# Solving DeltaNet's diagonal blocks on 128 partitions without DRAM

## The chip, the cores and the metric

One core of a Trainium2 chip runs the whole program. The metric is the time of one execution in device microseconds (us). The core has five engines that run side by side, each strictly in the order of its own instructions: TensorE (PE in the profile, with its weight loads as PEld), VectorE (DVE), ScalarE (ACT), GpSimd (POOL) and SyncE (SP), which here issues the loads of the weights. An instruction that needs another engine's result waits for a semaphore, and everything behind it on its engine waits too.

## What is computed

The reference is a trunk of four layers over 256 tokens with 1024 features: a pooling mixer, a gated DeltaNet, latent attention, and a pooling mixer again. The change lies in the second layer:

```python
L = jnp.where(strict, jnp.einsum('bhnid,bhnjd->bhnij', k_beta, k) * decay, 0.0)
A = jnp.eye(C, dtype=L.dtype) + L
rhs = jnp.concatenate([v_beta, k_beta * jnp.exp(g)[..., None]], axis=-1)
sol = lax.linalg.triangular_solve(A, rhs, left_side=True, lower=True)
...
attn = jnp.where(causal, jnp.einsum('bhnid,bhnjd->bhnij', q, k) * decay, 0.0)
```

There are 8 heads with keys of 128 and values of 256 numbers; q and k are the projection of the layer's input after a causal convolution over four tokens, a SiLU and a normalisation. The reference works in chunks of 64 tokens; the kernel in two of 128 (t = 0, 1), which gives the same result. So for each of 16 pairs of chunk and head a lower triangular matrix I + L of 128 x 128 has to be inverted or solved.

## The kernel before

**Projections.** `project` multiplies the layer's input with 512 columns of a weight matrix. `weights` loads two blocks of 128 rows at a time on SP's queue (L133, three `raw` buffers) and splits each block into a rounded part (`whi`, a cast on ACT, L149) and a rest (`wlo`, a subtraction on DVE, L150, or on POOL for the blocks named in `pool`); nine buffers of each are in use. PE then makes three products per block (L162). In the DeltaNet layer there are twelve such projections, which the list `order` (L673) strings together: g0 to g3 are gates, k0 and k1 keys, q0 and q1 queries, v0 to v2 values, V3 and c3 the two halves of the last values. d, a0, a1, s and i are the decays, the matrices L of four heads each (`lower`), the substitution and the inverses; u0 and u1 use the result.

**What happens to a projection.** DVE runs three taps of the convolution (L750) over PE's result, ACT starts it (L747) and closes with a SiLU (L787 for keys and queries, written to `kqT`; L902 for values). PE transposes the result into tokens by channels (L793, L906). For keys, DVE copies them to `ktok` (L799). `against` makes products of four heads with the keys (L806), and DVE multiplies each head with its scale and its decays `DT` (L813): this gives `LT`, L transposed, from the keys, and `attnT` from the queries.

**The solution.** `substitution` cuts each of the 16 matrices into four diagonal blocks of 32 x 32. Eight copies on SP's queue (L838) bring the 64 blocks from `LT` to DRAM (`d_l`), and one brings them back as `Lb` (L841), one block to a partition, so on 64 partitions. POOL then runs 31 pairs of steps (L846, L850): row r times the solved rows, subtracted from the rows below; the result is the inverse of the blocks, `Tb`. POOL's queue writes it to DRAM (`d_t`, L853) and reads it back in four copies onto the diagonal of `T` (L857). `inverses` puts the blocks together: DVE transposes T to `U` (L929), then PE, DVE and ACT run two stages, `pairs` (L938 to L947) and `whole` (L952 to L965), for t = 0 and 1, with small matmuls of 64 and 32 columns. `news` (L979) multiplies the values with U, and a chain over the heads ends the layer (L1004 to L1055), with the next projection, `layer_out`, beside it.

**Order.** The program is recorded in the order of the code and of the list `order`; a list scheduler then places the instructions of all engines by a model of their times, so an engine's instructions of neighbouring steps are interleaved. On the chip this order is fixed. Buffers are handed on in the same way: `kqT` of q1 is written into the buffer that `Lb` had, and waits for its last reader.

Of the kernel before, what the change touches and what calls it, by code (L numbers as in the profile page):

```python
# [42 lines left out]
def trunk(ctx: ExitStack, tc: tile.TileContext, x, positions, norm_g, pool_w_in, pool_w_grp,  # L43
# [566 lines left out]
    def gdn_setup():  # L610
# [35 lines left out]
        GC.update(utri=utri, maskT=maskT, m32=m32, half=half, tap=tap, bws=bws,  # L646
                  alog=alog, dtb=dtb)

    def gdn_layer(i, j, hT):
# [124 lines left out]
        def channels(dst, c0, hf, which):  # L774
# [13 lines left out]
            for c in range(0, 4, 2):  # L788
# [9 lines left out]
                if which == 0:  # L798
                    nc.vector.tensor_copy(ktok[:, h:h + 2, :], ps[:, 0])  # L799

        def against(dst, rhs, sf, hf, t):
# [3 lines left out]
            for b in range(4):  # L805
                nc.tensor.matmul(ps[:, b], lhsT=kT[hf][:, b, tt], rhs=rhs[hf][:, b, tt],  # L806
                                 start=True, stop=True)
            for b in range(4):
# [4 lines left out]
                nc.vector.scalar_tensor_tensor(  # L813
                    out=o, in0=v, scalar=sf[:, t, h:h + 1], in1=d, op0=ALU.mult, op1=ALU.mult)
# [17 lines left out]
        def substitution():

            d_l = dram.tile([M * Q, B * B], F32, name="d_l")
            lv = d_l.rearrange("(t m d) (r c) -> t d r m c", t=NT, d=Q, r=B)
            for t in range(NT):
                for d in range(Q):
                    nc.sync.dma_start(out=lv[t, d],  # L838
                                      in_=LT[t][d * B:(d + 1) * B, :, d * B:(d + 1) * B])
# [571 lines left out]
```

## Time and profile before

| | |
|---|---|
| median of 3 runs | 829.0 us (827.01 to 829.16) |
| profiled execution | 832.1 us, its span 830.4 us |
| mean clock of PE | 0.986 of full speed |
| instructions | 16162 |
| layer with the change | about 170 to 420 us of the span |

The span is the time from the first to the last instruction. Rows of the profile read: start and duration in us, engine, line of the kernel, operation, written and read tile, shapes, and how many such instructions were merged (x). In brackets stands how long the engine was idle before the instruction, and what it waited for. Rows of windows give the stretch, its length, then the busy time and the number of instructions of PE, PEld, DVE, ACT and POOL, and last PE's granted clock, the share of the DMA engines and their GB/s. Rows with `|` are groups: count, then busy time in us and the mean of one instruction in ns, then the idle time before them. PE's busy time contains overlaps, since matmuls are pipelined.

### The profile page before, as it was taken

What the parts mean: (1) busy time and instruction counts of PE and PEld (TensorE: products, weight loads), DVE (VectorE), ACT (ScalarE), POOL (GpSimd) and SP (SyncE); (2) the same over time, 40 slices, a digit from 0 to 9 for tenths busy, and PEclk for the clock granted to TensorE, in tenths of its full rate; (3) what the DMA queues carried; (4) which work ended last, traced back from release to release, by engine and by line L of the source; (5) the groups of instructions that cost most, each with busy time, mean ns of one, the idle gap of its engine ahead of it and who ended that gap; (6) DMA issues with size and microseconds to landing.
All of it is one profiled execution on the core that took longest, in us unless ns stands there. A gap on an engine that the chain in (4) does not pass through costs nothing.

```text
span 830.4 us, 16162 instructions
## 1 busy us (share of the span) xinstructions
PE 799.4 (96%) x5966; PEld 758.0 (91%) x5966; DVE 603.4 (73%) x1141; ACT 492.9 (59%) x993; POOL 159.8 (19%) x296
## 2 busy tenths in 40 slices
PE   8989999999898979999999999999999999999996
PEld 7989988989898978788989999999999989999996
DVE  4699887666987967356666678778877767877772
ACT  6665565567855655255566564666665565566662
POOL 2001100334236992023121112000000120000012
PEclk9999999999999989899999999999999999999998
DMA  6865666756655544303647786653552547576662
GB/s 204 224 180 167 193 209 210 221 153 195 193 135 180 163 139 118 124 12 115 187 125 224 231 180 185 192 164 102 153 175 80 179 143 214 183 223 202 202 204 51
DMA packets 109079, 139.90 MB, mean 168 GB/s; under 512 B 21316, under 2 KB 51208, under 8 KB 109000
## 3 DMA queue, kind: packets, MB, share of 16 engines
q1 hardware_dynamic: 106608, 137.12, 55.0%
q0 software_dynamic: 528, 1.58, 0.6%
q8 instruction: 47, 0.77, 0.4%
q10 hardware_dynamic: 1864, 0.17, 0.2%
q14 instruction: 32, 0.26, 0.1%
HBM read 137.27 MB, written 1.58 MB: 167 GB/s over the span
## 4 chain that ended last, share of the span: by engine, by line
PE 67%; DVE 11%; POOL 8%; DMA 8%; issue 4%; ACT 2%; SPq 0%; POOLq 0%; DVEq 0%; ACTq 0%
PE acc L162 53%; PE aux L162 7%; POOL pr L846 3%; DVE wlo L154 3%; POOL Tb L850 2%; DMA raw<-in_pool_w_out_dram 2%; DVE wlo L150 1%; DMA raw<-in_pool_w_in_dram 1%; DVE win L551 1%; DMA T<-d_t 1%; DMA Lb<-d_l 1%; DVE h L397 1%; DMA Gb<-d_g 1%; PE aux L979 1%; PE tp L1314 1%
## 5 line engine op out<-in xcount | busy, mean ns | idle before, releaser
L150 DVE TENSOR_TENSOR wlo<-raw,whi 128x512 fp32r<-128x512 f32 (+1 forms) x366 | 254.2, 719 | 104.3 <-ACT whi L149 100.8
L149 ACT CAST whi<-raw 128x512 fp32r<-128x512 f32 (+1 forms) x380 | 223.7, 617 | 167.6 <-PE acc L162 82.3
L162 PE MATMUL acc<-hTh,whi 128*128 128x256 f32 x832 | 230.7, 278 | 2.3 <-ACT gsg L670 1.5
L162 PE MATMUL acc<-hTl,whi 128*128 128x256 f32 x832 | 231.2, 278 | 0.0
L162 PE MATMUL acc<-hTh,wlo 128*128 128x256 f32 x832 | 229.8, 277 | 0.0
L162 PEld LDWEIGHTS acc<-hTh,whi 128*128 128x128 f32 x832 | 160.7, 193 | 2.9 <-ACT gsg L670 1.7
L162 PEld LDWEIGHTS acc<-hTl,whi 128*128 128x128 f32 x832 | 160.8, 193 | 0.3
L162 PEld LDWEIGHTS acc<-hTh,wlo 128*128 128x128 f32 x832 | 160.7, 193 | 0.1
L162 PE MATMUL acc<-wlo,yTh 128*128 128x256 f32 (+1 forms) x384 | 112.7, 312 | 0.8 <-DVE wlo L154 0.8
L162 PE MATMUL acc<-whi,yTh 128*128 128x256 f32 (+1 forms) x384 | 112.3, 315 | 0.0
L162 PE MATMUL acc<-whi,yTl 128*128 128x256 f32 (+1 forms) x384 | 89.1, 313 | 0.0
L162 PEld LDWEIGHTS acc<-wlo,yTh 128*128 128x128 f32 x384 | 73.2, 191 | 4.8 <-DVE wlo L154 1.7
L162 PEld LDWEIGHTS acc<-whi,yTh 128*128 128x128 f32 x384 | 72.9, 191 | 3.1
L162 PEld LDWEIGHTS acc<-whi,yTl 128*128 128x128 f32 x384 | 63.1, 191 | 3.4
L154 DVE SCALAR_TENSOR_TENSOR wlo<-raw,colsT,whi 128x512 fp32r<-128x512 f32 x64 | 47.0, 769 | 21.1 <-ACT whi L153 20.7
L153 ACT ACTIVATE whi<-raw,gain 128x512 fp32r<-128x512 f32 x64 | 43.6, 720 | 31.1 <-DMA raw<-in_pool_w_in_dram 22.6
L153 ACT ACTIVATE whi<-raw,colsT 128x512 fp32r<-128x512 f32 x64 | 43.5, 720 | 30.9 <-DMA raw<-in_pool_w_out_dram 18.0
L385 POOL TENSOR_TENSOR hg<-x,gain 128x256 f32<-128x256 f32 x16 | 13.4, 850 | 244.1 <-DVE x L450 244.1
L162 PE MATMUL acc<-wlo,hTh 128*128 128x512 f32 (+1 forms) x144 | 54.8, 385 | 1.9 <-DVE wlo L150 1.3
L154 DVE SCALAR_TENSOR_TENSOR wlo<-raw,gain,whi 128x512 fp32r<-128x512 f32 x64 | 46.6, 748 | 11.1 <-ACT whi L153 11.1
L162 PE MATMUL acc<-whi,hTh 128*128 128x512 f32 (+1 forms) x144 | 52.7, 379 | 0.7 <-ACT hTh L242 0.7
L162 PE MATMUL acc<-whi,hTl 128*128 128x512 f32 (+1 forms) x144 | 42.5, 373 | 0.0
(364 smaller groups left out, 1530.9 us busy)
## 6 DMA issues: line engine op xcount, KB each, us to landing
raw<-in_pool_w_in_dram SPq DMA_DIRECT2D x62, 512.0 KB, 4.4
raw<-in_gdn_w_in_dram SPq DMA_DIRECT2D x48, 512.0 KB, 4.0
raw<-in_pool_w_out_dram SPq DMA_DIRECT2D x32, 512.0 KB, 4.4
raw<-in_mla_w_in_dram SPq DMA_DIRECT2D x24, 512.0 KB, 4.5
raw<-in_mla_w_uq_dram SPq DMA_DIRECT2D x36, 256.0 KB, 3.4
raw<-in_pool_w_grp_dram SPq DMA_DIRECT2D x16, 512.0 KB, 3.8
raw<-in_gdn_w_out_dram SPq DMA_DIRECT2D x16, 512.0 KB, 3.8
raw<-in_mla_w_ukv_dram SPq DMA_DIRECT2D x32, 256.0 KB, 3.3
```

The lines of the kernel that those rows point to most:

```text
L149: a = nc.scalar.copy(hi, v)
L150: b = e.tensor_tensor(out=lo, in0=v, in1=hi.bitcast(F32), op=ALU.subtract)
L153: a = nc.scalar.activation(hi, v, AF.Copy, scale=g)
L154: b = e.scalar_tensor_tensor(out=lo, in0=v, scalar=g, in1=hi.bitcast(F32), op0=ALU.mult, op1=ALU.subtract)
L162: return nc.tensor.matmul(inorder(o, n), lhsT=lhs, rhs=woven(rhs, n), start=start, stop=stop)
L385: nc.gpsimd.tensor_tensor(out=self.early[t, a], in0=xs[t][:, sl], in1=self.g[:, sl], op=ALU.mult)
L397: nc.vector.scalar_tensor_tensor(out=h[:, cut:], in0=xs[t][:, sl], scalar=r[:, 0:1], in1=self.g[:, sl], op0=ALU.mult, op1=ALU.mult)
L551: nc.vector.tensor_tensor(out=nxt[:, :, d:], in0=cur[:, :, d:], in1=cur[:, :, :S - d], op=ALU.add)
L846: nc.gpsimd.tensor_tensor(out=pv, op=ALU.mult, in0=Lb[:, r, r + 1:, None].to_broadcast([M * Q, n, c]), in1=Tb[:, r:r + 1, :c].to_broadcast ...
L850: mark["blocks"] = nc.gpsimd.tensor_tensor(out=tv, in0=tv, in1=pv, op=ALU.subtract).ins
L979: nc.tensor.matmul(ps[:, c], lhsT=U[0][:, h, :], rhs=vR[h // 2][:, 0, c * DV:(c + 1) * DV], start=True, stop=True)
L1314: nc.tensor.transpose(ps[:, a * P:(a + 1) * P], sb[:, a * P:(a + 1) * P], ident)
```

## The change

The blocks are gathered, solved and put back without DRAM. `lower` copies the diagonal blocks of each four heads, as they are made, to a tile `Lg`: for t = 0 on POOL, for t = 1 on ACT. One transpose on DVE makes `Lb` from it, with every block on two partitions, so that 128 are used and each partition solves half of the block's columns (16 of 32). The steps on POOL are still 31 pairs, over half as many columns. A second transpose on DVE turns the result, and four copies, two on ACT and two on POOL, put it on the diagonal of `T`. The start value needs a small table, `which`, made once.

Beside this: the keys' copies to `ktok` go from DVE to ACT; the queries' products are multiplied with `DT` four heads at a time, without the keys' scale, which is moved to later instructions (s2 in place of s1, and DT alone for ktok); the splits on POOL for v0 (four) and g2 (two) go to DVE; and `i` moves in the list ahead of v2.

```diff
-                            pool=((0, 4), (7,), (3, 7), (7,))[vi])
+                            pool=((0, 4), (7,), (), (7,))[vi])
-        order = "g0 k0 d a0 g1 k1 a1 s q0 v0 v1 v2 q1 V3 i c3 g2 u0 u1 g3".split()
+        order = "g0 k0 d a0 g1 k1 a1 s q0 v0 v1 i v2 q1 V3 c3 g2 u0 u1 g3".split()
...
-        Tb = big("Tb", B, B)[:M * Q]
+        C = B // 2
+        solve = big("solve", 2, B, C)
+        Tb, turned_ = solve[:, 0], solve[:, 1]
         nc.gpsimd.memset(Tb, 0.0)
-        nc.gpsimd.memset(Tb.rearrange("m r c -> m (r c)")[:, ::B + 1], 1.0)
+        for a in range(2):
+            nc.gpsimd.tensor_copy(Tb.rearrange("p r c -> p (r c)")[:, a * C::B + 1],
+                                  which[:, a, :C])
+        Lg = small("Lg", M, B, bufs=1)
...
-                    nc.vector.tensor_copy(ktok[:, h:h + 2, :], ps[:, 0])
+                    nc.scalar.copy(ktok[:, h:h + 2, :], ps[:, 0])
...
+            if sf is None:
+                hs = slice(4 * hf, 4 * hf + 4)
+                nc.vector.tensor_tensor(out=dst[t][:, hs, :], in0=ps, in1=DT[t][:, hs, :],
+                                        op=ALU.mult)
+                return
...
         def lower(hf):
             for t in range(NT):
                 against(LT, kT, s2, hf, t)
+                hs = slice(4 * hf, 4 * hf + 4)
+                for d in range(Q):
+                    dd = slice(d * B, (d + 1) * B)
+                    o = Lg[dd, t * H + 4 * hf:t * H + 4 * hf + 4]
+                    if t:
+                        nc.scalar.copy(o, LT[t][dd, hs, dd])
+                    else:
+                        nc.gpsimd.tensor_copy(o, LT[t][dd, hs, dd])
 
         def substitution():
-            d_l = dram.tile([M * Q, B * B], F32, name="d_l")
-            lv = d_l.rearrange("(t m d) (r c) -> t d r m c", t=NT, d=Q, r=B)
-            for t in range(NT):
-                for d in range(Q):
-                    nc.sync.dma_start(out=lv[t, d],
-                                      in_=LT[t][d * B:(d + 1) * B, :, d * B:(d + 1) * B])
-            Lb = big("Lb", B, B)[:M * Q]
-            nc.sync.dma_start(out=Lb, in_=d_l.rearrange("m (r c) -> m r c", r=B))
-            pr = small("pr", 256, bufs=1)[:M * Q]
+            Lb = big("Lb", B, B)
+            nc.vector.transpose(Lb, Lg.rearrange("p m c -> p c m")[:, :, None, :].to_broadcast(
+                [P, B, 2, M]))
+            pr = small("pr", 136, bufs=1)
             for r in range(B - 1):
-                n, c = B - 1 - r, r + 1
+                n, c = B - 1 - r, r // 2 + 1
                 pv = pr[:, :n * c].rearrange("m (a b) -> m a b", a=n)
                 nc.gpsimd.tensor_tensor(out=pv, op=ALU.mult,
-                                        in0=Lb[:, r, r + 1:, None].to_broadcast([M * Q, n, c]),
-                                        in1=Tb[:, r:r + 1, :c].to_broadcast([M * Q, n, c]))
+                                        in0=Lb[:, r + 1:, r:r + 1].to_broadcast([P, n, c]),
+                                        in1=Tb[:, r:r + 1, :c].to_broadcast([P, n, c]))
                 tv = Tb[:, r + 1:, :c]
                 mark["blocks"] = nc.gpsimd.tensor_tensor(out=tv, in0=tv, in1=pv,
                                                          op=ALU.subtract).ins
-            d_t = dram.tile([M * Q, B * B], F32, name="d_t")
-            nc.gpsimd.dma_start(out=d_t.rearrange("m (r c) -> m r c", r=B), in_=Tb)
-            tv = d_t.rearrange("(m d) (r c) -> d r m c", d=Q, r=B)
+            nc.vector.transpose(turned_.rearrange("p r c -> p (r c)"),
+                                Tb.rearrange("p r c -> p c r"))
+            tv = turned_.rearrange("p r c -> p (r c)").rearrange("p (c m) -> p m c", m=M)
             for d in range(Q):
                 dd = slice(d * B, (d + 1) * B)
-                nc.gpsimd.dma_start(out=Ts[dd, :, :, dd].rearrange("p t h c -> p (t h) c"),
-                                    in_=tv[d])
+                o = Ts[dd, :, :, dd].rearrange("p t h c -> p (t h) c")
+                if d % 2:
+                    nc.scalar.copy(o, tv[dd])
+                else:
+                    nc.gpsimd.tensor_copy(o, tv[dd])
...
-                against(at_, qT, rk, hf, t)
+                against(at_, qT, None, hf, t)
...
-                            pool=((1, 3, 5, 7), (), (), ())[vi])
+                            pool=())
...
-                                         scale=s1[:, 0, h:h + 1])
+                                         scale=s2[:, 0, h:h + 1])
...
-            v2[h] = worka("v2", DV)
-            nc.scalar.activation(v2[h], ps[:, :DV], AF.Copy, scale=s1[:, 1, h:h + 1])
+            nc.scalar.activation(v2[h], ps[:, :DV], AF.Copy, scale=s2[:, 1, h:h + 1])
```

How the instructions stand on the engines (line numbers are those of each kernel; in the changed one the lines behind 630 are higher). The end of the substitution on POOL before: the last pair of steps, then work on the queries (`Gb`, `rq`), the copy to DRAM, and behind a split the four copies back.

```order
L846 TENSOR_TENSOR pr<-Lb,Tb 64x31
L850 TENSOR_TENSOR Tb<-Tb,pr 64x31
L878 TENSOR_TENSOR Gb<-Gb,kqT 128x512
L879 TENSOR_SCALAR rq_2510<-ssq 128x2x4
L853 DMA d_t<-Tb 64x1024
L928 MEMSET X_4169 128x8x32
L772 TENSOR_TENSOR rq<-rq_2510,halves 128x2x4
L150 TENSOR_TENSOR wlo<-raw,whi 128x512
L857 DMA T<-d_t 32x16x32 x4
```

The same place on POOL in the changed kernel; `solve` holds Tb and its transpose.

```order
L863 TENSOR_TENSOR pr<-Lb,solve 128x16
L867 TENSOR_TENSOR solve<-solve,pr 128x16
L896 TENSOR_TENSOR Gb<-Gb,kqT 128x512
L897 TENSOR_SCALAR rq_2519<-ssq 128x2x4
L783 TENSOR_TENSOR rq<-rq_2519,halves 128x2x4
L878 COPY T<-solve 32x16x32 x2
```

The two DMAs and the split are gone; the two copies to T stand behind the same work on the queries.

DVE before, where T comes back, at the end of the second queries: U's transposes stand behind the products of q1 (`attnT`) and ahead of the convolution of the last values (`vc`).

```order
L150 TENSOR_TENSOR wlo<-raw,whi 128x512 x2
L813 SCALAR_TENSOR_TENSOR attnT<-aux,rk,DT 128x128 x7
L797 TENSOR_REDUCE ssq<-sq 128x2x2
L813 SCALAR_TENSOR_TENSOR attnT<-aux,rk,DT 128x128
L929 STREAM_TRANSPOSE U<-T 128x1024 x2
L750 SCALAR_TENSOR_TENSOR vc<-acc,tap,vc 128x255
```

DVE in the changed kernel, at the end of the convolution of v2 (`vc_3910`, `vc_3927`): the transpose of the solution stands ahead of v2's last taps; splits and the first taps of q1 (`cv_4083`) follow, then U's transposes.

```order
L869 STREAM_TRANSPOSE solve_2506<-solve_2506 128x512
L756 SCALAR_TENSOR_TENSOR vc_3910<-acc_3771,tap_645,vc_3910 128x253
L150 TENSOR_TENSOR wlo_4212<-raw_4210,whi_4213 128x512
L756 SCALAR_TENSOR_TENSOR vc_3927<-acc_3772,tap_645,vc_3927 128x253
L150 TENSOR_TENSOR wlo_4216<-raw_4210,whi_4217 128x512
L150 TENSOR_TENSOR wlo_4246<-raw_4244,whi_4247 128x512
L150 TENSOR_TENSOR wlo_4250<-raw_4244,whi_4251 128x512
L756 SCALAR_TENSOR_TENSOR cv_4083<-acc_3944,tap_645,cv_4083 128x255
L150 TENSOR_TENSOR wlo_4317<-raw_4315,whi_4318 128x512
L756 SCALAR_TENSOR_TENSOR cv_4083<-acc_3944,tap_645,cv_4083 128x254
L947 STREAM_TRANSPOSE U_3661<-T_2511 128x1024
L947 STREAM_TRANSPOSE U_3662<-T_2511 128x1024
```

U's transposes moved ahead of most of q1's convolution, and a wait for POOL's last step now stands in front of v2's last taps.

PE before, behind the last projection of the layer (g3): the second half of the inverses in one piece, then the values' products.

```order
L162 MATMUL acc<-whi,hTl_2253 128x512 x2
L962 MATMUL aux<-U,X 64x64 x8
L952 MATMUL aux<-ident,U 64x64 x8
L956 MATMUL aux<-T,LT 128x64 x8
L962 MATMUL aux<-U,X 64x64 x8
L979 MATMUL aux<-vR,U 128x256 x8
L1006 MATMUL aux<-u_4405,ktok 128x256 x2
```

PE in the changed kernel, twelve matmuls before the end of g3's projection: the last piece of the inverses, then q1's products and the first of the values' products.

```order
L162 MATMUL acc<-whi,hTl_2260 128x512 x2
L980 MATMUL aux<-U,X 64x64 x8
L817 MATMUL aux<-kqT 128x128 x8
L997 MATMUL aux<-vR,U 128x256 x2
L162 MATMUL acc<-whi,hTh_2259 128x512
L162 MATMUL acc<-wlo,hTh_2259 128x512
```

The small matmuls of the inverses now stand between matmuls of V3, g2 and g3.

More of the change, by code (lines that the diff above doesn't have):

```diff
@@ L625, in gdn_setup @@
         nc.gpsimd.memset(half, -0.5)
+        cols = workb("cols", 2, 32)
+        for a in range(2):
+            nc.gpsimd.memset(cols[:, a, :16], 1.0 - a)
+            nc.gpsimd.memset(cols[:, a, 16:], float(a))
+        which = const.tile([P, 2, 32], F32, name="which")
+        nc.vector.transpose(which.rearrange("p a c -> p (a c)"), cols.rearrange("p a c -> p (a c)"))
         crow = workb("crow", P)
@@ L645, in gdn_setup @@
         nc.scalar.dma_start(out=dtb, in_=gdn_dt_bias[0:1, :].to_broadcast([P, GDN_H]))
-        GC.update(utri=utri, maskT=maskT, m32=m32, half=half, tap=tap, bws=bws,
+        GC.update(utri=utri, maskT=maskT, m32=m32, half=half, which=which, tap=tap, bws=bws,
                   alog=alog, dtb=dtb)
@@ L653, in gdn_layer @@
         w_in = gdn_w_in[j]
-        utri, maskT, m32, half, tap, bws, alog, dtb = (
-            GC[n] for n in ("utri", "maskT", "m32", "half", "tap", "bws", "alog", "dtb"))
+        utri, maskT, m32, half, which, tap, bws, alog, dtb = (
+            GC[n] for n in ("utri", "maskT", "m32", "half", "which", "tap", "bws", "alog", "dtb"))
         def sc(name):
@@ L755, in gdn_layer @@
         Q, B = 4, 32
-        Tb = big("Tb", B, B)[:M * Q]
+        C = B // 2
+        solve = big("solve", 2, B, C)
+        Tb, turned_ = solve[:, 0], solve[:, 1]
         nc.gpsimd.memset(Tb, 0.0)
-        nc.gpsimd.memset(Tb.rearrange("m r c -> m (r c)")[:, ::B + 1], 1.0)
+        for a in range(2):
+            nc.gpsimd.tensor_copy(Tb.rearrange("p r c -> p (r c)")[:, a * C::B + 1],
+                                  which[:, a, :C])
+        Lg = small("Lg", M, B, bufs=1)
         Ts = big("T", NT, H, P)
@@ L768, in gdn_layer @@
             sc(n) for n in ("rk", "rki", "rq", "rq2", "s1", "s2"))
-        kds, neG = (small(n, H, bufs=1) for n in ("kds", "neG"))
+        neG = small("neG", H, bufs=1)
         def power(o, a):
@@ L807, in against @@
                                  start=True, stop=True)
+            if sf is None:
[3 more added lines that the diff above has]
+                return
             for b in range(4):
                 h = 4 * hf + b
-                o, v, d = dst[t][:, h, :], ps[:, b], DT[t][:, h, :]
-                if dst is LT:
-                    o, v, d = inorder(o), inorder(v), woven(d)
                 nc.vector.scalar_tensor_tensor(
-                    out=o, in0=v, scalar=sf[:, t, h:h + 1], in1=d, op0=ALU.mult, op1=ALU.mult)
+                    out=inorder(dst[t][:, h, :]), in0=inorder(ps[:, b]), scalar=sf[:, t, h:h + 1],
+                    in1=woven(DT[t][:, h, :]), op0=ALU.mult, op1=ALU.mult)
         LT = [big("LT", H, P) for _ in range(NT)]
@@ L851, in substitution @@
                                                          op=ALU.subtract).ins
-            d_t = dram.tile([M * Q, B * B], F32, name="d_t")
-            nc.gpsimd.dma_start(out=d_t.rearrange("m (r c) -> m r c", r=B), in_=Tb)
-            tv = d_t.rearrange("(m d) (r c) -> d r m c", d=Q, r=B)
+            nc.vector.transpose(turned_.rearrange("p r c -> p (r c)"),
+                                Tb.rearrange("p r c -> p c r"))
+            tv = turned_.rearrange("p r c -> p (r c)").rearrange("p (c m) -> p m c", m=M)
             for d in range(Q):
                 dd = slice(d * B, (d + 1) * B)
-                nc.gpsimd.dma_start(out=Ts[dd, :, :, dd].rearrange("p t h c -> p (t h) c"),
-                                    in_=tv[d])
+                o = Ts[dd, :, :, dd].rearrange("p t h c -> p (t h) c")
[3 more added lines that the diff above has]
+                    nc.gpsimd.tensor_copy(o, tv[dd])
             nc.vector.reciprocal(rki, rk)
-            nc.vector.tensor_tensor(out=kds, in0=rk[:, 0, :], in1=DT[0][:, :, P - 1],
-                                    op=ALU.mult)
             nc.vector.tensor_scalar(neG, eG[:, 1, :], -1.0, None, ALU.mult)
             nc.gpsimd.tensor_tensor(out=ktok, in0=ktok, op=ALU.mult,
-                                    in1=kds[:, :, None].to_broadcast([P, H, P]))
+                                    in1=DT[0][:, :, P - 1:].to_broadcast([P, H, P]))
         at_ = []
```

## The prediction

> **What bounds the kernel now.** I read the page first, then the windows of 50 us, then the gaps of PE, and last what POOL, DVE, ACT and SP do around them.
>
> ```profile
> span 830.4 us, 16162 instructions
> PE 799.4 (96%) x5966; PEld 758.0 (91%) x5966; DVE 603.4 (73%) x1141; ACT 492.9 (59%) x993; POOL 159.8 (19%) x296
> ```
>
> PE is busy for 96% and its instructions stay the same, so only PE's gaps and PE's clock can give time back. The change touches the DeltaNet layer alone, which lies at about 170 to 420 us:
>
> ```profile
> 200.00:250.00 50.00, 46.82 (x393) 45.60 (x392) 43.13 (x102) 33.08 (x60) 17.83 (x17) 1.00 0.57 169
> 250.00:300.00 50.00, 42.14 (x357) 41.40 (x356) 42.52 (x82) 29.60 (x63) 39.99 (x60) 0.96 0.57 170
> 300.00:350.00 50.00, 47.24 (x318) 43.14 (x319) 30.82 (x56) 22.17 (x43) 15.70 (x23) 0.91 0.41 127
> 350.00:400.00 50.00, 49.91 (x248) 43.13 (x247) 28.16 (x61) 28.05 (x78) 11.40 (x32) 0.96 0.22 71
> ```
>
> The first number after the window's length is PE's busy time, the one behind the brackets PE's clock. PE lacks 3.2 + 7.9 + 2.8 + 0.1 = 14.0 us here, and the clock lost 50 x (0.04 + 0.09 + 0.04) = 8.5 us. That is 22.5 us in all: the most that the change can return. Where the gaps are (idle time in brackets, with its releaser):
>
> ```profile
> 220.84 0.38 PE L162 MATMUL acc<-hTh,whi 128*128 128x256 f32 x1 [1.48 <-ACT gsg L670]
> 228.09 0.44 PE L793 MATMUL tp<-ident,kqT 128*128 128x128 f32 x2 [1.18 <-ACT kqT L787]
> 253.11 0.44 PE L793 MATMUL tp<-ident,kqT 128*128 128x128 f32 x2 [1.19 <-ACT kqT L787]
> 270.83 0.66 PE L906 MATMUL tp<-ident,vc 128*128 128x128 f32 x4 [1.98 <-ACT vc L902]
> 300.83 0.69 PE L793 MATMUL tp<-ident,kqT 128*128 128x128 f32 x2 [4.69 <-ACT kqT L787]
> 344.80 2.00 PE L956 MATMUL aux<-T,LT 64*128 64x64 f32 x16 [0.67 <-ACT T L953]
> 347.58 1.97 PE L962 MATMUL aux<-U,X 64*64 64x64 f32 x16 [0.79 <-DVE X L959]
> ```
>
> The clock (the third number from a row's end) fell behind the longer ones and in the run of small matmuls:
>
> ```profile
> 270.00:280.00 10.00, 9.17 (x68) 9.17 (x69) 10.00 (x19) 8.00 (x17) 9.14 (x12) 0.83 0.56 166
> 290.00:300.00 10.00, 6.14 (x56) 5.95 (x54) 7.01 (x13) 4.89 (x12) 8.82 (x16) 0.95 0.56 164
> 300.00:310.00 10.00, 9.17 (x61) 9.17 (x62) 6.70 (x13) 5.84 (x12) 9.68 (x15) 0.71 0.32 85
> 340.00:350.00 10.00, 8.55 (x69) 7.46 (x68) 4.00 (x7) 2.33 (x4) 0.00 (x0) 0.84 0.31 107
> 350.00:360.00 10.00, 9.91 (x38) 8.00 (x37) 3.36 (x8) 5.17 (x12) 0.00 (x0) 0.82 0.00 0
> ```
>
> Two of the gaps have the old solution behind them:
>
> ```profile
> ACT kqT L787 <- POOL pr L846: 5.5, 1, 5.5
> 251.59 1.14 ACT L149 CAST whi<-raw 128x512 fp32r<-128x512 f32 x2 [2.43 <-DMA raw<-in_gdn_w_in_dram]
> 252.63 0.43 ACT L787 ACTIVATE kqT<-cv 128x256 f32<-128x256 f32 x1
> 243.70 3.79 SPq L838 DMA_DIRECT2D d_l<-LT  x8
> ```
>
> ACT cannot write the second queries' `kqT` until POOL has finished with `Lb` (a buffer handed on), and so PE stands 4.69 us at 300.83. And SP held a weight load behind its eight waiting `d_l` copies; ACT waits 2.43 us for weights in front of the `kqT` for which PE waits at 253.11.
>
> **The change, part by part.** First POOL's substitution, since everything after hangs on its end:
>
> ```profile
> 255.39 0.23 POOL L846 TENSOR_TENSOR pr<-Lb,Tb 64x31 f32<-64x31 f32 x1 [14.55 <-DMA Lb<-d_l]
> 255.70 0.26 POOL L850 TENSOR_TENSOR Tb<-Tb,pr 64x31 f32<-64x31 f32 x1
> ```
>
> A large step that met no split of DVE, the last of the 62 steps, then DVE's splits alone in the stretch of the substitution, and two splits in a quiet stretch:
>
> ```profile
> 272.30 0.62 POOL L846 TENSOR_TENSOR pr<-Lb,Tb 64x247 f32<-64x247 f32 x1
> 300.39 0.24 POOL L850 TENSOR_TENSOR Tb<-Tb,pr 64x31 f32<-64x31 f32 x1
> 255.40:300.60 45.20, 21.32 (x24) 0.94 0.52 156
> 393.19 1.28 DVE L150 TENSOR_TENSOR wlo<-raw,whi 128x512 fp32r<-128x512 f32 x2
> ```
>
> From 31 to 247 elements a step grows by (0.62 - 0.23)/216 = 0.0018 us per element on a base of 0.17; with 0.07 between two, 62 steps cost 62 x 0.24 + 0.0018 x elements. Before: 2 x 5456 elements, 14.9 + 19.6 = 34.5 us; it took 45.2. The missing 10.7 lie beside DVE's 24 splits (the window row holds L150 on DVE alone), 0.45 each; a split itself averages 21.32/24 = 0.89 there against 0.64 where POOL is quiet, so the two hinder each other. After: 2 x 2856 elements, 14.9 + 10.3 = 25.2; I count 19 splits between DVE's two transposes, which enclose the solution: 8.6. Together 34 us. (128 partitions cost no more than 64: see `Gb`, 128x512, below: 1.27, the formula's 1.09 and a little.)
>
> Its start:
>
> ```profile
> 238.94 1.90 POOL L863 TENSOR_TENSOR ktok<-ktok,kds 128x1024 f32<-128x1024 f32 x1 [0.29 <-DVE kds L860]
> 242.56 2.14 DVE L813 SCALAR_TENSOR_TENSOR LT<-aux,s,DT 128x128 f32<-128x128 f32 x8
> 300.60 1.27 POOL L878 TENSOR_TENSOR Gb<-Gb,kqT 128x512 f32<-128x512 f32 x1
> 303.48 1.85 POOL L772 TENSOR_TENSOR rq<-rq,halves 128x8 f32<-128x8 f32 x1
> 314.95 2.37 DVE L929 STREAM_TRANSPOSE U<-T 128x1024 f32<-128x1024 f32 x2 [3.06 <-DMA T<-d_t]
> ```
>
> Before, LT ended at 244.7 and the first step came 10.7 later. After, `ktok` (1.90) stands on POOL in front of the power that LT needs, and DVE carries v0's four splits itself: LT ends at about 248. ACT's block copies follow a cast for v2, whose buffer PE frees when it leaves v0 (253.11 less 21 matmuls of 0.11 and the gap: 249.6); four copies to 251, one transpose of 1.2: POOL starts at 252.4, 3 us earlier than before, and ends at 252.4 + 34 = **286.4** instead of 300.6.
>
> Its way back: the transpose of 512 columns 0.65, then POOL's two copies behind `Gb` 1.27, a small one (0.5) and the power 1.85. The copies are not in the trace. Rows that bound them:
>
> ```profile
> L1217 POOL CAST cknh<-ckTh 128x512 fp32r<-128x512 f32 x2 | 1.5, 730 | 23.8 <-ACT ckTh L244 23.8
> L953 ACT COPY T<-aux 64x512 f32<-64x512 f32 x2 | 1.2, 579 | 1.3 <-PE aux L952 1.3
> L799 DVE COPY ktok<-tp 128x256 f32<-128x256 f32 x4 | 1.6, 412 | 0.0
> L813 DVE SCALAR_TENSOR_TENSOR attnT<-aux,rk,DT 128x128 f32<-128x128 f32 x16 | 4.5, 338 | 0.0
> L940 DVE TENSOR_TENSOR X<-aux,m 128x512 f32<-128x512 f32 x2 | 1.4, 680 | 0.0
> ```
>
> On POOL a 512-column copy lies between `Gb`'s 1.27 and the cast's 0.73; I take 0.73. T is whole at 286.4 + 3.6 + 1.5 = 291.5 (292.6 with 1.27), against 314.9 before, when DVE's U could start. An ACT copy costs between nothing, where ACT waits anyway, and 0.58; a block copy of 128 columns I take at 0.35, the row's share for a quarter of the columns and the fixed part.
>
> Now PE. DVE and ACT work strictly in order, and both come to an instruction that waits for POOL's end: DVE to the second transpose, ACT to the copies of T. Behind DVE's stand the last taps of v2's convolution, and behind them PE's transposes for v2. DVE's own work between the transposes is 19 splits, 34 taps of the convolution (0.40 each, six in 2.43) and four more of 0.6. Three splits come before DVE must wait for the queries' transposes (256.4: 253.11 less its gap, 25 matmuls of 0.11 more, 2 for transposes and squares); the rest is 16 x 0.89 + 34 x 0.40 + 3 x 0.6 = 29.6, so it arrives at 286.0, just ahead of POOL's end. PE's v2 transposes go at 286.4 + 0.65 + 0.4 for a tap + 0.6 for the SiLU = **288.1**; PE itself could be there at 290.08 - 1.2 - 2.0 - 1.7 = 285.2, without the gaps at 253.11 and 270.83 and the lost clock. Before, and the six taps:
>
> ```profile
> 290.08 0.60 PE L906 MATMUL tp<-ident,vc 128*128 128x128 f32 x4
> 224.82 2.43 DVE L750 SCALAR_TENSOR_TENSOR cv<-acc,tap,cv 128x254 f32<-128x254 f32 x6
> ```
>
> So **-2.0** here. From there to q1's transposes PE has work, then at 300.83 the old gap of **-4.7** is gone: q1's `kqT` no longer takes `Lb`'s buffer. PE's first product with T comes at about 292, with T or just behind it (0.6 us if the copies are slow). The clock: 0.05 + 0.29 of ten us returns (**-3.4**), but the new gap of 2.9 us before 288 is longer than the one of 1.98 which was followed by 1.7 us lost at 0.83, so **+1.7**. The tail: the second half of the inverses stands before as one run without projections and is now spread over V3, g2 and g3: **-1.5** for its two gaps, **-3.4** for 0.16 and 0.18 of ten us.
>
> Costs: ACT's four `ktok` copies (1.6) and eight block copies (2.8) replace DVE's; the first two fall into ACT's waits for weights, the block copies come ahead of k1's convolution: **+0.5**. Six more splits on DVE, 3.8 us, and two transposes, 1.9, stand against 1.6 (`ktok`) and 16 x 0.34 - 4 x 0.68 = 2.7 (products): +1.4 on DVE, inside the wait for POOL. The scale s2 in place of s1 and the setup's five small instructions: nothing. If that cover fails, DVE's 1.4 is the price.
>
> Sum: -2.0 - 4.7 - 3.4 + 1.7 - 1.5 - 3.4 + 0.5 = **-12.8 us**. The profiled execution took 832.1 (span 830.4) and would take 819.3; on the median of 829.0 that is **816**.
>
> [...]
>
> **The rivals.**
> *The clock stays whole* at 288: none of the gaps of 1.2 and 1.5 us lowered it. 829 - 14.5 = 814.5. Chance 0.10.
> *Columns read with a stride.* POOL now reads a column of `Lb` 128 bytes apart. L850's first step reads such rows too: 0.26 against 0.23, 0.001 us per element, 2.9 us over 2856. Then 819. Against it: the 0.03 may be the start of a row, of which there are 496, 0.5 us. Chance 0.10. [...]
> *POOL is later* by 5 to 8 us, since each step holds off a split more often: each us past 286 goes straight to PE. 821 to 824. Chance 0.10.
> *All of it goes*, gaps and clock: 829 - 22.5 = 806.5. The gaps at 220 and 228, which ACT's order makes and the change leaves, speak against it. Chance 0.07.
> [...] 826.5 to 831.5. Chance 0.10.
> *Slower*: each of the 62 steps pays the 0.45, not only 19: 25.2 + 27.9 = 53 us. POOL ends at 305.5, DVE, ACT and PE all stand behind it, since now both wait in order where before only a `kqT` did: +19 on the sum, 835. It decides from 34 + 12.8 + 2.5 = 49 us on. Against it: DVE has no more splits in that stretch. Chance 0.11.
>
> **How the numbers follow.** Forecast 816, its own range 812 to 820, chance 0.42. Faster by over 0.3% (2.5 us, about what a measurement of this kernel tells from no change): 0.42 + 0.10 + 0.10 + 0.10 + 0.07 = 0.79; same 0.10; slower 0.11. The range of 809 to 828 leaves out "all", "slower" and a little of "same".
>
> **What would show it.** The substitution at 32 to 36 us for 62 steps, begun at 251 to 254; no gap of PE over 1 us at q1's transposes, one of 2 to 3 at v2's; the two transposes of DVE with under 2 us of waiting; the small matmuls between projections and a clock of 1.00 at 335 to 350. Wrong if POOL needs over 40, or if PE waits at the first product with T.

## The result, and the profile after

The changed kernel takes 820.5 us (median of 4 runs, 820.0 to 823.2), the kernel before 828.8 on the same chip (4 runs, 827.0 to 829.2): a ratio of 0.9904, interval 0.988 to 0.9928, or 8.3 us less. The prediction was 816.0 with a range of 809 to 828 and a sum of -12.8 us. The direction and the range held; four and a half of the 12.8 us did not come.

The page of the changed kernel, span and busy time of each engine:

```profile
span 818.3 us, 16144 instructions
PE 793.2 (97%) x5966; PEld 754.2 (92%) x5966; DVE 599.4 (73%) x1133; ACT 499.8 (61%) x1007; POOL 144.9 (18%) x300
```

The two profiled executions differ by 12.1 us of span, which looks like the predicted 12.8. It is not that. The timelines of PE give two marks which both kernels have: the first transposes of k0's `kqT` (call this moment A), ahead of all that the change touches, and the first product of the closing chain with `ktok`, behind all of it. Before:

```profile
207.88 0.44 PE L793 MATMUL tp<-ident,kqT 128*128 128x128 f32 x2 [0.52 <-ACT kqT L787]
...
355.04 1.03 PE L1006 MATMUL aux<-u,ktok 128*128 128x256 f32 x4
```

After, with the two gaps of PE over 0.9 us that lie between the marks (in brackets, with the releaser):

```profile
204.58 0.38 PE L804 MATMUL tp<-ident,kqT 128*128 128x128 f32 x2
...
217.16 0.38 PE L162 MATMUL acc<-hTh,whi 128*128 128x256 f32 x1 [1.16 <-ACT gsg L676]
...
286.86 1.11 PE L924 MATMUL tp<-ident,vc 128*128 128x128 f32 x4 [7.79 <-ACT vc L920]
...
342.62 1.03 PE L1024 MATMUL aux<-u,ktok 128*128 128x256 f32 x4
```

From mark to mark it is 147.16 us before and 138.04 after: **9.1 us** less. The other 3 us were gone before A, where both kernels run the same code but for a few small instructions of the setup; A lies between 204.6 and 209.2 in all the kernels below, so that part is the spread of single executions. Times below are therefore told as distances from A where two kernels are compared. Between the marks, too, one execution differs from the next: before_own_lb below, whose median is that of the kernel before, has 144.18 from mark to mark. A difference of 3 us there needs the ratios beside it.

The windows of 50 us (length, PE, PEld, DVE, ACT and POOL busy, PE's clock, DMA) say the same in another way:

```profile
200.00:250.00 50.00, 48.75 (x424) 48.05 (x423) 44.82 (x101) 39.82 (x81) 17.21 (x24) 1.00 0.62 190
250.00:300.00 50.00, 42.21 (x357) 42.02 (x355) 40.19 (x81) 30.88 (x63) 35.28 (x68) 0.90 0.47 142
300.00:350.00 50.00, 49.91 (x326) 43.99 (x325) 28.93 (x53) 24.93 (x53) 5.29 (x8) 1.00 0.33 111
350.00:400.00 50.00, 50.00 (x298) 45.05 (x297) 32.62 (x64) 29.56 (x78) 13.91 (x34) 1.00 0.37 119
```

PE lacked 14.0 us and 8.5 us of clock before; it lacks 9.1 and 5.0 now, 8.4 less together. Nearly all that is left sits in one row, 250 to 300: the gap of 7.79, and 5.0 of clock, some of which falls into the gap itself and costs nothing there. What stands behind that gap is read from the timelines of three engines. POOL, the first and the last step of the substitution, and its copies to `T`:

```profile
247.72 0.60 POOL L863 TENSOR_TENSOR pr<-Lb,solve 128x31 f32<-128x31 f32 x1 [3.48 <-DVE Lb L857]
...
282.68 0.22 POOL L867 TENSOR_TENSOR solve<-solve,pr 128x16 f32<-128x16 f32 x1
...
286.42 2.55 POOL L878 COPY T<-solve 32x512 f32<-32x512 f32 x2
```

DVE, the last tap of v2 that it could do, and the transpose of the solution behind it:

```profile
274.45 0.47 DVE L756 SCALAR_TENSOR_TENSOR vc<-acc,tap,vc 128x254 f32<-128x254 f32 x1
282.94 1.04 DVE L869 STREAM_TRANSPOSE solve<-solve 128x512 f32<-128x512 f32 x1 [8.01 <-POOL solve L867]
283.91 0.43 DVE L756 SCALAR_TENSOR_TENSOR vc<-acc,tap,vc 128x253 f32<-128x253 f32 x1
```

ACT, the copies to `T` and behind them the SiLU of v2:

```profile
284.01 2.14 ACT L876 COPY T<-solve 32x512 f32<-32x512 f32 x2 [9.08 <-DVE solve L869]
286.18 0.63 ACT L920 ACTIVATE vc<-vc 128x512 f32<-128x512 f32 x1
```

Read it from the end: PE's transposes wait for a SiLU on ACT. ACT came to it late, since two copies of the solution stand ahead of it. They wait for DVE's transpose, which waits for POOL's last step at 282.90. DVE had stood at that transpose since 274.9, with two taps of v2 behind it. So POOL's end still sets when PE goes on; only the place has moved, from q1's transposes to v2's.

The clock in windows of 10 us: the gap, what follows it, and the stretch of the small matmuls, where 0.84 stood before:

```profile
280.00:290.00 10.00, 3.14 (x15) 3.14 (x16) 5.30 (x9) 5.95 (x11) 9.14 (x18) 0.62 0.18 52
290.00:300.00 10.00, 10.00 (x83) 10.00 (x82) 9.97 (x19) 5.92 (x13) 0.06 (x1) 0.87 0.47 135
...
340.00:350.00 10.00, 9.91 (x46) 8.27 (x46) 5.29 (x11) 6.50 (x17) 0.42 (x2) 1.00 0.16 53
```

### The profile page after: what moved, and what is told of

Same layout as the page of the kernel before. It is cut to its first block, busy times and chain, and to the rows that moved or that the text cites. A ratio compares the mean times of both kernels' runs of the same rounds, so it can differ in the third digit from the quotient of the medians.

```text
span 818.3 us, 16144 instructions
## 1 busy us (share of the span) xinstructions
PE 793.2 (97%) x5966; PEld 754.2 (92%) x5966; DVE 599.4 (73%) x1133; ACT 499.8 (61%) x1007; POOL 144.9 (18%) x300
## 4 chain that ended last, share of the span: by engine, by line
PE 83%; POOL 5%; DVE 5%; issue 2%; ACT 2%; DMA 2%; SPq 0%; POOLq 0%; ACTq 0%; DVEq 0%
PE acc L162 67%; PE aux L162 8%; POOL solve L867 2%; POOL pr L863 2%; DVE wlo L150 1%; DVE cv L756 1%; DVE h L397 1%; PE tp L1332 1%; DMA x<-in_x_dram 1%; DMA raw<-in_pool_w_in_dram 1%; ACT whi L149 0%; DMA raw<-in_gdn_w_in_dram 0%; PE aux L974 0%; PE tp L1070 0%; PE aux L817 0%
```

## The experiments

Twelve kernels were run, each beside the kernel before. Two theories stood against each other at first. **The waiters:** PE's 7.79 us hang on where DVE's transpose and ACT's copies are written; put them behind v2's work and the time returns. **The floor:** POOL's end is simply too late for the work that PE has, and whoever is freed at one place stands at the next. In the diffs, `later(x, y)` makes the scheduler place what is written under it behind the instructions x and y; `mark` remembers such instructions.

### The transpose and ACT's copies behind v2 (turn_late)

```diff
-        order = "... s q0 v0 v1 i v2 q1 V3 c3 g2 u0 u1 g3".split()
+        order = "... s q0 v0 v1 v2 t i q1 V3 c3 g2 u0 u1 g3".split()
...
+            elif name == "t":
+                with later(mark["silu"], mark["tap"]):
+                    turns()
```

`turns()` holds the second transpose and the four copies; the marks are v2's last tap on DVE and its last SiLU on ACT.

> The changed kernel, but DVE's second transpose stands behind v2's last tap and ACT's two copies of T behind v2's last SiLU; everything else of the change is kept. Theory A (PE's 7.79 us at v2's transposes come from these three instructions standing in front of v2's taps and SiLU while they wait for POOL's end at 282.9): that gap goes. In this order PE's first product with T comes 29 matmuls behind v2's last transposes, so PE is there at about 284.6, T is whole at 289, and a gap of 4 to 5 us appears there: 820.5 - 7.8 + 4.4 = 817 (816 to 819). Rival B (PE has nothing to do before POOL's end anyway, since its next weights queue behind the same instructions): 820 to 822.

Measured: 822.5 against 830.9, ratio 0.9895 (0.9876 to 0.9914), the same as the change itself (0.9904). v2's transposes went at once, and PE stood at the first product with `T`. PE's timeline:

```profile
279.55 0.60 PE L928 MATMUL tp<-ident,vc 128*128 128x128 f32 x4
...
291.94 3.67 PE L960 MATMUL aux<-T,LT 128*128 128x64 f32 x16 [7.44 <-POOL T L880]
```

And its clock in two windows of 10 us:

```profile
280.00:290.00 10.00, 4.50 (x41) 4.31 (x39) 3.25 (x5) 3.73 (x6) 8.72 (x19) 0.96 0.18 51
290.00:300.00 10.00, 8.06 (x40) 8.06 (x41) 8.54 (x15) 4.72 (x12) 2.58 (x5) 0.53 0.41 110
```

A gap of 7.44 instead of 7.79: the wait moved by one place and kept its size. A miss for the waiters, as they stood. But the gap is made of other parts now. PE came to `T` at 284.50, and POOL's last step ended at 285.11, only 0.6 us later. The other 6.8 us are the way back, and 4.7 of them are POOL's work on the queries, which stands ahead of its copies to `T`:

```profile
285.07 1.27 POOL L900 TENSOR_TENSOR Gb<-Gb,kqT 128x512 f32<-128x512 f32 x1
...
289.75 2.14 POOL L880 COPY T<-solve 32x512 f32<-32x512 f32 x2
```

ACT's two copies were done at 288.4. POOL's copies ahead of the work on the queries were not tried.

### The inverses later too (turn_late_inv_late)

turn_late, with the first product with T put behind part of q1 and V3:

```diff
-        order = "... v2 t i q1 V3 c3 g2 u0 u1 g3".split()
+        order = "... v2 t q1 V3 i c3 g2 u0 u1 g3".split()
...
-                with later(mark["strip"], mark["dve"]):
+                with later(*splits[-8]):
                     inverses()
```

> As turn_late, and the inverses' products with T queue behind V3's first weights, 103 matmuls behind v2's last transposes instead of 29. Theory A: PE comes to the first product with T at about 292, T is whole at 289, DVE's splits go on at 284 and ACT's casts at 286, before PE needs them at about 288. No gap over 1 us is left at 275 to 300, and the 5.0 us of clock lost there return as well: 820.5 - 7.8 - 5.0 = 808 (807 to 812). Rival B (weights queue behind the same waits): the gap moves to PE's projections at about 285 to 290, 815 to 821.

Measured: ratio 0.9913 (0.9892 to 0.9934), a second miss. PE now stood at q1's transposes, where it stood before the change. It came there at 287.7, 2.1 us behind the end of POOL's last step (285.65), and waited for what DVE and ACT, which had stood 7 us for that end, still had to do for q1:

```profile
293.96 0.69 PE L805 MATMUL tp<-ident,kqT 128*128 128x128 f32 x2 [6.23 <-ACT kqT L799]
```

### The order of before with the new solution (old_order)

```diff
-        order = "... s q0 v0 v1 i v2 q1 V3 c3 g2 u0 u1 g3".split()
+        order = "... s q0 v0 v1 v2 q1 V3 i c3 g2 u0 u1 g3".split()
```

> The changed kernel with the list of steps of before (the inverses behind V3). By my account of the change the two gaps of the tail (1.5 us) and the clock behind them (3.4 us) come back: 820.5 + 4.9 = 825.4 (824 to 827). Rival (the place of the inverses carries nothing, the faster solution alone made the gain): 820 to 821.

Measured: ratio 0.993 (0.9906 to 0.9954), some 2.2 us more than the change by the ratios, though the intervals overlap; mark to mark 140.80 against 138.04. The gap at v2 stayed (7.68). The small matmuls ran without projections again, and there the clock fell:

```profile
340.00:350.00 10.00, 9.21 (x54) 7.71 (x53) 2.67 (x4) 3.43 (x8) 0.00 (x0) 0.83 0.25 84
```

So moving `i` in the list is worth 2 to 3 us, less than the 4.9 of the sum: with `T` there early, only one of the tail's two gaps comes back (0.79 at 343.67).

### All four copies on POOL (pool_copies)

```diff
-                if d % 2:
-                    nc.scalar.copy(o, tv[dd])
-                else:
-                    nc.gpsimd.tensor_copy(o, tv[dd])
+                nc.gpsimd.tensor_copy(o, tv[dd])
```

> The changed kernel with all four copies of T on POOL. ACT's two copies (2.14 us) no longer stand in front of v2's SiLU, so the gap at v2 falls from 7.8 to 5.6 us; but POOL needs 2.55 us more and T is whole at 291.6 instead of 289.0, where PE's first product with T comes at about 288. Theory A: both count, PE waits there for T, net 1.6 us slower: 822 (821 to 823). Rival C (ACT's copies alone set the time): 2.1 us faster, 818.4.

Measured: ratio 0.9894 (0.9876 to 0.9912). From POOL's last step, which ended at 287.37, to v2's transposes it took 2.2 us instead of 3.96, so ACT's copies were on the path with 1.8 us. But POOL ended 1.7 later from A in this execution, and the gap was about the old one; nor did PE wait where `T` was whole later. The timelines of PE and of POOL:

```profile
289.59 1.12 PE L921 MATMUL tp<-ident,vc 128*128 128x128 f32 x4 [7.52 <-ACT vc L917]
```

```profile
290.89 5.20 POOL L875 COPY T<-solve 32x512 f32<-32x512 f32 x4
```

The way is shown, its worth in time is not: neither number of its expectation came.

### Half of the steps (half_steps_late)

```diff
-            for r in range(B - 1):
+            for r in range(0, B - 1, 2):
```

> turn_late with the same order on PE, DVE and ACT, but every second of POOL's 31 steps of the substitution is left out (16 remain, so T is not the inverse): POOL's part falls from 35 to about 18 us and ends near 268. Theory B of now (wherever DVE's second transpose stands, what is queued behind it waits for POOL's end, and PE with it): the 7.4 us in front of the first product with T go, and the 4.7 us of clock behind them: 12 us less than turn_late, about 0.975 of the time before (0.972 to 0.979), 808 on the scale of 828.8. Rival (DVE's and ACT's own queues set that point, not POOL): 0.985 to 0.99.

Measured: 814.2 against 830.4, ratio 0.9799 (0.9775 to 0.9823). This kernel leaves out every second pair of steps, so its `T` is not the inverse; it only times the wait. POOL ended at 269.0 and PE had no gap over 0.9 us between 200 and 400. The two windows that follow turn_late's above:

```profile
280.00:290.00 10.00, 9.53 (x87) 9.34 (x86) 9.02 (x14) 9.29 (x18) 3.44 (x4) 1.00 0.52 154
290.00:300.00 10.00, 10.00 (x100) 10.00 (x99) 9.49 (x19) 5.05 (x11) 1.29 (x1) 1.00 0.53 160
```

With the same order as in turn_late, only less work on POOL, the whole stop is gone: it hangs on POOL's end, and not on DVE's and ACT's own queues. The run doesn't part the floor from the waiters, since the waiters wait for that same end. It returned 8.0 us (0.9895 - 0.9799 of 831), not the expected 12. Read as windows, turn_late lost 7.4 in the gap and 4.7 of clock (0.47 of ten). But the clock's share counts idle time too: PE worked at half rate from 291.94 to 299.4 (0.21 us from one product of the projection to the next, 0.11 behind it), so the clock cost 3.7. And PE came to v2's transposes 1.7 us later here (74.05 behind A against 72.32).

### The transpose inside q1, and behind it (turn_in_q1, turn_behind_q1)

If PE has no work behind v2 that is free of POOL, q1's projection might be that work. Both put the transpose and the copies behind taps of q1's convolution, and the inverses behind V3:

```diff
+        order = "... s q0 v0 v1 v2 q1 t V3 i c3 g2 u0 u1 g3".split()
...
+                with later(mark["tap0"], mark["kq0"]):
+                    turns()
```

In turn_behind_q1 the marks are tap1 and kq1, those of q1's second half.

> The changed kernel, complete, with DVE's second transpose behind the taps of the first half of q1's projection and ACT's copies behind that half's SiLU, the inverses behind V3's fifth weights. There DVE and ACT arrive at about 285, when POOL ends, and nobody waits for it. If POOL's end only costs what stands idle behind it: no gap over 1.5 us at 275 to 300, T whole at about 291, PE at the first product with T at 293: 820.5 - 7.8 - 5.0 = 808, ratio 0.975 (0.972 to 0.981). Rival (the work has to wait in any case; q1's second half stands behind the transpose): a gap of 3 to 6 us at q1's transposes, 0.985 to 0.992.

> As turn_in_q1, but behind all of q1's taps and SiLUs, 5 to 6 us later. T whole at about 295, PE's first product with T at 296: no gap in front of v2 and q1, 0.975 (0.972 to 0.981). Rival (T is then late for the inverses, whose small matmuls fall into the stretch without projections): the clock at 330 to 350 falls below 0.9 and 2 to 5 us come back, 0.978 to 0.985.

Measured: ratios 0.9959 (0.994 to 0.9977) and 0.9898 (0.9875 to 0.992). In both, ACT stood at v2's `vR` for a step of POOL that reads `Lb`. turn_in_q1, timelines of ACT and of PE:

```profile
287.37 0.84 ACT L934 ACTIVATE vR<-tp,rki 128x256 f32<-128x256 f32 x2 [6.12 <-POOL pr L866]
```

```profile
288.26 0.58 PE L163 MATMUL acc<-hTh,whi 128*128 128x256 f32 x1 [5.07 <-ACT vR L934]
```

And turn_behind_q1:

```profile
285.45 0.84 ACT L934 ACTIVATE vR<-tp,rki 128x256 f32<-128x256 f32 x2 [6.55 <-POOL pr L866]
```

```profile
288.63 0.69 PE L807 MATMUL tp<-ident,kqT 128*128 128x128 f32 x2 [4.80 <-ACT kqT L799]
```

`vR` had been handed the buffer in which `Lb` lay. (turn_in_q1 was 9.2 us faster from mark to mark, but only 3.4 by the ratio: behind the closing mark its execution took 480.5 us, the one before 475.4. Why stays open.)

### Lb in a buffer of its own (four kernels)

So a new suspicion: the buffer alone. In the kernel before it can be tested without any other part of the change, since there q1's `kqT` waited for `Lb` (4.69 us). before_own_lb and before_lb are the kernel before with one edit each; turn_behind_q1_lb and turn_in_q1_lb put `Lb` into T's tile in the two kernels above:

```diff
 before_own_lb
-            Lb = big("Lb", B, B)[:M * Q]
+            Lb = small("Lb", B, B, bufs=1)[:M * Q]
 before_lb
-        Ts = big("T", NT, H, P)
+        TL = big("T", NT + 1, H, P)
+        Ts = TL[:, :NT]
...
-            Lb = big("Lb", B, B)[:M * Q]
+            Lb = TL[:M * Q, NT].rearrange("p h (a c) -> p (h a) c", c=B)
```

> The kernel before with one edit: its Lb lies in a buffer of its own, which q1's kqT does not take over. By my account the 4.69 us in front of q1's transposes go and most of the 2.9 us of clock behind them: 828.8 - 4.7 - 2.9 = 821.2, ratio 0.991 (0.989 to 0.994), which would be nearly all that the whole change brought. Rival (another wait for POOL stands right behind, Gb's product or T): 0.996 to 1.001.

> The kernel before, with Lb in a buffer that lives as long as T, which nothing takes over before the inverses. (In before_own_lb v2's vR took it over in place of q1's kqT, and PE stood 6.4 us.) By my account of the change the 4.69 us at q1's transposes go and most of the 2.9 us of clock behind them: 0.991 (0.989 to 0.994), nearly the whole gain of the change with the old solution kept. Rival (it isn't the buffer: the time is POOL's, and something else waits): 0.996 to 1.001.

> turn_behind_q1, with Lb in a buffer that lives as long as T, so that v2's vR (or q1's kqT) does not take it over. In turn_behind_q1 ACT stood 6.55 us at vR for POOL's last read of Lb, and PE 4.8 us behind it. Theory B': the price of POOL's end is paid by whoever has to wait for it, DVE, ACT or a buffer; with all three taken away the 4.8 us and 3.4 us of clock at 280 to 300 go: 0.990 - 0.010 = 0.980 (0.977 to 0.983), about 812 on the scale of 828.8. The tail's gaps and clock (about 4 us at 330 to 350) stay. Rival (a further wait for POOL stands behind): 0.987 to 0.991.

> turn_in_q1 with Lb in a buffer that lives as long as T. Theory B': the 5.1 us behind vR go and 3.4 us of clock; DVE comes to the transpose at about 285, within 1 us of POOL's end, and T is whole some 5 us sooner than in turn_behind_q1_lb, so the tail is better by up to 3 us: 0.977 to 0.985. Rival: DVE arrives before POOL's end and q1's second half waits 2 to 4 us: 0.985 to 0.99.

Measured: 1.0006 (0.9988 to 1.0023), 1.001 (0.9992 to 1.0028), 0.9935 (0.9914 to 0.9956) and 0.9994 (0.9977 to 1.001): four misses, and the last two made their kernels slower by 0.0035 to 0.0037, at the edge of the intervals. before_own_lb, timelines of ACT and of PE:

```profile
297.42 0.84 ACT L909 ACTIVATE vR<-tp,rki 128x256 f32<-128x256 f32 x2 [7.11 <-POOL pr L846]
```

```profile
300.60 0.69 PE L793 MATMUL tp<-ident,kqT 128*128 128x128 f32 x2 [6.38 <-ACT kqT L787]
```

before_lb, the same two:

```profile
301.92 0.43 ACT L788 ACTIVATE kqT<-cv 128x256 f32<-128x256 f32 x1 [9.83 <-POOL Gb L879]
```

```profile
302.40 0.69 PE L794 MATMUL tp<-ident,kqT 128*128 128x128 f32 x2 [9.67 <-ACT kqT L788]
```

In the first, whose pools hand their buffers on in another order, v2's `vR` waits for POOL's steps. In the second, `kqT` takes the buffer of q0's `kqT`, which POOL releases with `Gb`, the instruction right behind the last step. turn_behind_q1_lb and turn_in_q1_lb went the second way as well. ACT of turn_behind_q1_lb, and PE of turn_in_q1_lb:

```profile
289.26 0.84 ACT L935 ACTIVATE vR<-tp,rki 128x256 f32<-128x256 f32 x2 [9.46 <-POOL Gb L904]
```

```profile
289.97 1.12 PE L932 MATMUL tp<-ident,vc 128*128 128x128 f32 x4 [8.46 <-ACT vc L928]
```

The name in the brackets changes from kernel to kernel; PE stands 4.7 to 9.7 us each time.

### Work that is free of POOL (gate_ahead_of_v2)

If it is a floor, PE must be given work that needs nothing of the solution. The gate projection g2 is such work. turn_late with g2 moved:

```diff
-        order = "... s q0 v0 v1 v2 t i q1 V3 c3 g2 u0 u1 g3".split()
+        order = "... s q0 v0 v1 g2 v2 t i q1 V3 c3 u0 u1 g3".split()
```

> turn_late, complete, with one more move in the list of steps: the gates' third projection (g2, about 11 us of PE that needs neither POOL nor q0's or Lb's buffers) stands ahead of v2 instead of near the end. DVE's second transpose is still behind v2's last tap, which now comes at about 288, and v2's vR, which takes Lb's buffer over, at about 290; POOL's last step ends at 283 to 285, so none of the three routes (DVE's order, T, a buffer) meets it any more. Theory (only POOL's end against PE's position counts): no gap over 1.5 us at 270 to 300 and a clock of 1.00 there, as in half_steps_late, which gave 0.980: 0.980 (0.976 to 0.985). Rival (g2 was the cover of the inverses' small matmuls; without it their gaps and the clock at 330 to 360 come back, 4 to 8 us): 0.985 to 0.992.

Measured: 817.85 against 831.14, ratio 0.9845 (0.9815 to 0.9875), the best of the complete kernels. Its windows of 10 us, two at the old gap and one in the tail:

```profile
280.00:290.00 10.00, 10.00 (x92) 10.00 (x91) 9.41 (x20) 6.75 (x13) 8.67 (x19) 1.00 0.57 167
290.00:300.00 10.00, 10.00 (x92) 10.00 (x92) 7.10 (x10) 8.50 (x17) 6.93 (x9) 1.00 0.45 151
...
330.00:340.00 10.00, 10.00 (x50) 9.13 (x49) 2.06 (x4) 2.92 (x8) 0.00 (x0) 0.66 0.00 0
```

PE never stood at POOL's end, though POOL ended 82.2 us behind A, later than in any other kernel with the new solution: its last step, and DVE's transpose, which no longer waits:

```profile
289.39 0.59 POOL L867 TENSOR_TENSOR solve<-solve,pr 128x16 f32<-128x16 f32 x1
```

```profile
290.22 1.08 DVE L871 STREAM_TRANSPOSE solve<-solve 128x512 f32<-128x512 f32 x1
```

One move did two things here: PE has work, and DVE comes later to its transpose; the run doesn't part them. g2 is then missing in the tail, where the small matmuls stand with less between them: the clock falls to 0.66 for ten us, about 3.4. From mark to mark it is 131.55 against 137.76 in turn_late.

## Why the prediction was right, and where its sum failed

**POOL's work: right.** Predicted 34 us for the substitution and an end 78.5 us behind A (286.4 less 207.9); it took from 247.72 to 282.90, 35.2 us, and ended 78.3 behind A. That the end is only 0.2 off is in part luck: the start, at 43.1 behind A, had been put at 44.5, and the steps took 1.2 longer. The splits of DVE cost 7.6 us instead of 8.6; the steps without them 27.6 instead of 25.2, in part because the formula goes by the multiplications alone, and the subtractions were longer before too (0.42 against 0.37 for 112 elements). The two rivals that lengthen POOL's part, "POOL is later" and "slower", did not occur. The strided read cost little, 0.03 us in a step of 136 elements, see below.

**The way back: this step failed.** The prediction put "286.4 + 0.65 + 0.4 for a tap + 0.6 for the SiLU = 288.1" between POOL's end and v2's transposes, 1.65 us. It took 3.96 (286.86 less 282.90): the transpose 1.04, and ACT's two copies 2.14 in front of the SiLU. The prediction had ACT's copies in its text, even in the sentence on who waits in order, but bounded each by 0 to 0.58 and let none of it into this sum. So the term "-2.0" became +0.1: v2's transposes came 82.2 us behind A before, and 82.3 after. All that PE gains up to that point it loses there.

**PE's gap at v2: 2.9 predicted, 7.8 measured.** 2.1 of the difference is the way back (82.3 against 80.2 from A). 2.8 is that PE itself was ready earlier, 74.5 behind A instead of 77.3; that part moves no end, it only makes the gap longer. DVE too was ready 8 us before POOL, not "just ahead of POOL's end": its splits beside POOL cost 0.69, not 0.89, which is 3.2 of the 8; the rest was not taken apart.

**q1's gap: right.** None over 1 us was left there: -4.7, as predicted. But the reason given, that `kqT` no longer takes `Lb`'s buffer, was only the route. With the buffer changed and POOL as slow as before, nothing came (1.0006 and 1.001). PE was free at q1 because POOL ended 78 instead of 93 us behind A.

**The clock: two terms mis-sized.** The prediction took the clock's loss as share times window. In windows of 1 us the clock fell to 0.50 while PE still stood (299 to 300 before, 283 to 286 after, with PE at 0.00), which costs nothing, and was still at 0.50 when PE worked again. Before, at the end of the stretch behind q1's gap:

```profile
304.00:305.00 1.00, 1.00 (x7) 1.00 (x7) 0.96 (x3) 0.26 (x1) 1.00 (x1) 0.50 0.94 197
305.00:306.00 1.00, 1.00 (x7) 1.00 (x7) 0.30 (x1) 0.78 (x2) 1.00 (x2) 0.61 0.01 0
```

After, inside the new gap and at the end of the stretch behind it:

```profile
284.00:285.00 1.00, 0.00 (x0) 0.00 (x0) 1.00 (x3) 0.99 (x1) 0.83 (x3) 0.50 0.00 0
...
292.00:293.00 1.00, 1.00 (x8) 1.00 (x7) 1.00 (x2) 0.78 (x2) 0.00 (x0) 0.66 0.64 246
```

So PE worked at half rate from 300.83 to 305.8 before, and from 286.86 to 292.6 after; half of that time is lost. The -3.4 at q1 came to -2.5, and the +1.7 behind the new gap to +2.8.

**The tail: right.** The small matmuls do lie between projections and their clock is 1.00. Before, they cost 1.5 for the two gaps and 3.0 for 6.0 us at half rate (347.58 to 353.6): -4.5 instead of -4.9.

Sum: +0.1 - 4.7 - 2.5 + 2.8 - 4.5 = -8.8, against -12.8; from mark to mark it is -9.1. The predicted costs of +0.5 were not measured by themselves. PE stood at v2 longer than it had at q1 (7.79 against 4.69), though POOL was on time. The gain that is left is PE's shorter way from v2 on. (The range of 809 to 828 leaves out most of "same", 828 to 831.5 of 826.5 to 831.5, and not a little of it.)

**What the runs show of the cause.** The change works by POOL's earlier end, and 2 to 3 us by the list. Of the 14.4 us by which POOL ends earlier from A (92.7 before), 10.0 are the shorter steps and 4.4 the earlier start; no run has the steps on 128 partitions without the way around DRAM, or the reverse, so the two are parted by these rows alone. POOL's end remained a limit that PE met by five routes: DVE's order, `T` itself, `Lb`'s buffer through `vR` or `kqT`, and q0's buffer through `Gb`. Moving waiters or buffers left a stop in each case; shortening POOL (0.9799) or giving PE free work (0.9845) removed it. How much of a stop is POOL's end and how much the way back differs: PE came 3.8 us ahead of that end in the changed kernel, 0.6 in turn_late, and 2.1 behind it in turn_late_inv_late. Not tried: POOL's copies to `T` ahead of the work on the queries, part of the rows on DVE, the smaller parts of the change by themselves (`ktok` on ACT, the splits on DVE), and the kernel before with only `i` moved.

## What to carry to other kernels

When an engine with a long chain is late, count how much work the bound engine has that needs nothing of that chain; moving the instruction or the buffer at which it waits, in eight kernels here, only changed the name in the brackets. On an engine that works in order, add every instruction between the awaited one and the one that the bound engine needs, with its own duration, also those that "wait anyway". Count a lower clock only while the engine works. And compare two profiles from a mark that both share, not by their spans.
